# Expert weights of a hybrid encoder layer: one stream in long rows instead of 384 separate blocks

## The chip, the cores and the metric

The kernel runs on one core of one Trainium2 chip. A core has a matrix engine (PE, with its weight loads shown apart as PEld), a vector engine (DVE), a scalar engine (ACT), GpSimd (POOL), a sync engine (SP) that here mostly issues transfers, and 16 DMA engines that move data between HBM and the on-chip memory of 128 partitions. The metric is the device time of one execution in microseconds, lower is better. Before the change the runs gave 1816.92, 1818.54 and 1820.82 us, with a median of 1818.54 us.

## What is computed

One layer of a bidirectional encoder on 256 tokens of width 2048, all in float32. A mixing part (a Hyena group, a grouped-query attention group, an output projection) is followed by a layer norm, and then by 16 experts, each of which picks its own 32 tokens. The weights of the experts are most of the data: 16 experts x 3 matrices x 2048 x 1536 x 4 bytes are 604 MB, and each is used once.

```python
x = layer_norm(DN_ALPHA * x + jnp.einsum('ble,ed->bld', mixed, w_out), ln1_g, ln1_b)
# expert_choice_moe:
aff = jax.nn.softmax(logits, axis=-1)
gate, idx = lax.top_k(aff.transpose(0, 2, 1), C)          # C = 32 tokens for each expert
xg = x[bi, idx]
h = jax.nn.silu(jnp.einsum('becd,edf->becf', xg, w_gate)) * jnp.einsum('becd,edf->becf', xg, w_up)
y = jnp.einsum('becf,efd->becd', h, w_down) * gate[..., None]
return jnp.zeros_like(x).at[bi, idx].add(y.astype(x.dtype))
# and last
x = layer_norm(DN_ALPHA * x + moe, ln2_g, ln2_b)
```

## The kernel before

**Stages.** Up to about 400 us the mixing part runs: projections with PE busy nearly all the time, whose weights (`win`, `wo`) come through a ring of three slots (`ring_a`). Then come the moments of the first layer norm (`moments`, L739), the router's softmax (L759 to 768), the search for the top 32 (L790 to 801) and the one-hot matrices (`onehot`). From about 415 us the 16 experts follow (`expert`, L885): gate and up (`proj`, L867), then down (the loop from L917), and at the end the second layer norm.

**Blocks.** The weights of the experts are cut into blocks of [128, 3072] float32, 1.5 MB each: 8 for gate, 8 for up and 8 for down of each expert, 24 x 16 = 384. One block is one DMA: each of the 128 partitions gets one contiguous row of 12 KB. PE reads a gate or up block with 8 matmuls of 32x384 for each of two row pairs (L881; the profile counts 16), a down block with 12 (L929, counted 24) and then 2 (L936, counted 4). On odd experts the gathers of the next pair (L831) stand between the down blocks.

**Slots.** A block goes into a slot that `slot()` (L161) takes in turn from a list of 13: four of `ring_b`, four of `ring_d`, three of `ring_a`, two of `ring_c` (L736). The 14th place of the first round is half of a `big` buffer (`extra`, L718). Each pool turns over its own buffers: a new tile waits until PE has read the old one. Two other users take slots too. `row_tiles` (L838) puts two rows of the first layer norm into one, and `rw` (L952), the rows of the second layer norm for the end of the program, holds one of `ring_a`'s three from its allocation ahead of the last expert until the end.

**Order.** All weight DMAs stand on SP's queue (L592, L653, L875, L923, L925). SP works strictly in order: where one DMA waits for its slot, all behind it wait too. There are eight completion semaphores for DMAs of SP, used in turn, so that the ninth DMA also waits until the first has landed. The last down block of the last expert is fetched in two halves of 512-byte pieces (L923).

```python
rings[:] = [ring_b] * RB + [ring_d] * RD + [ring_a] * RA + [ring_c] * RC_
...
rw = slot(FR)[:, :D]
...
w = slot()
Q.dma_start(w, a[nm][e, s])
```

Of the kernel before, what the change touches and what calls it, by code (L numbers as in the profile page):

```python
# [10 lines left out]
F32 = mybir.dt.float32  # L11
FR = mybir.dt.float32r
AF = mybir.ActivationFunctionType
# [3 lines left out]
D = 2048  # L17
# [11 lines left out]
OUT_CHUNKS = [(0, 384), (384, 384), (768, 384), (1152, 384), (1536, 256), (1792, 256)]  # L29
EG = 2  # L30
MAGIC = 12582912.0
KL = OUT_CHUNKS[-1][0] // 128
RA = 3
RB = 4
RD = 4
RC_ = 2
NSPLIT = 4
AHEAD = 2
FSTEP = 3
EXTRA = 4  # L40
ROPE_LAG, SOFT_LAG = 3, 2
# [4 lines left out]
def constants():  # L46
# [31 lines left out]
    return np.ascontiguousarray(mix), np.ascontiguousarray(embt), np.ascontiguousarray(base)  # L78


def layout(i):
# [34 lines left out]
    for g in (n["q_norm"], n["k_norm"]):  # L116
# [11 lines left out]
                                for a, b in OUT_CHUNKS], 2))  # L128
    for k in ("w_gate", "w_up"):
        o[k] = c(n[k].reshape(E, 8, 2, 128, FF).transpose(0, 1, 3, 2, 4).reshape(E, 8, 128, SLOT))  # L130
    o["w_down"] = c(n["w_down"].reshape(E, 12, 128, 8, 256).transpose(0, 3, 2, 1, 4).reshape(E, 8, 128, SLOT))
    o["rows"] = c(np.stack([n["ln1_g"], n["ln1_b"], n["ln2_g"], n["ln2_b"]]).reshape(1, 4 * D))
# [3 lines left out]
ORDER = ["mixc", "base", "xt", "xr", "win", "bqkv", "par", "nrm", "ffn", "emb", "w3", "dec", "wo",  # L136
         "w_gate", "w_up", "w_down", "rows"]


def body(tc, a, out, upto=None):  # L140
# [7 lines left out]
    per = main.enter_context(tc.tile_pool(name="per", bufs=1, side="left"))  # L148
    ring_a = main.enter_context(tc.tile_pool(name="ra", bufs=RA, side="left"))
    s1b = ExitStack()  # L150
# [6 lines left out]

    rings = [ring_a]
    state = {"n": 0}

    def slot(dt=F32):  # L161
        p = rings[state["n"] % len(rings)]
        state["n"] += 1
        return p.tile([128, SLOT], dt, name="w", tag="w")

# [420 lines left out]

    pre = {}

    def ahead(pool):
        i = len(pre)  # L590
        w = pre["w_gate", i] = pool.tile([128, SLOT], F32, name="w", tag="w")
        Q.dma_start(w, a["w_gate"][0, i])  # L592

    gts, done = {}, set()
# [12 lines left out]
    for i in range(NCT + 4):  # L607
        if i == 1:
            Q.dma_start(wt[1][1], a["win"][1, 1])
        elif i:  # L610
            load_win(i)
        if i == NCT - 1:
            rope_tables()
        if i < NCT:
            side.append(first_filters() if i == 0 else filters(i))
        box = []
        for _ in hy_proj(i, box) if i < NCT else qkv_proj(i - NCT, box):
            tick()
        while len(side) > (1 if i == 0 else 0) and i < NCT + 3:
            tick()  # L620
        side.append(hy_mix(i, box) if i < NCT else qkv_post(i - NCT, box))
        if i == NCT:
            s1h.close()
            ring_b = main.enter_context(tc.tile_pool(name="rb", bufs=RB, side="right"))
        elif i > NCT:
            ahead(ring_b)
    res = big().rearrange("p (t d) -> p t d", t=2)
# [70 lines left out]
    for half in (0, 1):  # L698
        for ci, (c0, cn) in enumerate(OUT_CHUNKS):
            if half == 1 and ci == 0:  # L700
                while side:
                    tick()
                token_rms(sqa, 1)
                s1a.close()
                ring_d = main.enter_context(tc.tile_pool(name="rd", bufs=RD, side="right"))
            ps = [bank([128, 512], f"ip{t}") for t in range(2)]
# [6 lines left out]
            if half == 0 and ci == 0:  # L713
                ahead(ring_b)
            if half == 0 and ci == 3:
                room = big()
                spare = room[:, SLOT:].rearrange("p (n t) -> p n t", t=L)
                extra = pre["w_up", EXTRA] = room[:, :SLOT]  # L718
                Q.dma_start(extra, a["w_up"][0, EXTRA])
            for t in range(2):  # L720
# [145 lines left out]

    def proj(e, nm, tag, step=None):  # L867
        xg = xgs[e // EG]
        c0 = (e % EG) * CAP
        p = bank([128, 512], tag)  # L870
        for s in range(8):
            w = pre.pop((nm, s), None)
            if w is None:
                w = slot()
                Q.dma_start(w, a[nm][e, s])  # L875
            if step:
# [8 lines left out]
    def expert(e):  # L885
        step = None
        if e == 0:
# [7 lines left out]
        pg_ = proj(e, "w_gate", "ip0", step)  # L895
        h = pm_.tile([128, 384], F32, name="h")
        S.activation(h, pg_, AF.Silu)  # L897
        pu_ = proj(e, "w_up", "ip1")
        V.tensor_tensor(h, h, pu_, op=ALU.mult)  # L899
# [15 lines left out]
        acc = accs[0]  # L915
        last = e == n_exp - 1
        for n in range(8):  # L917
            w = slot()
            pieces = [(0, 128), (128, 256)] if last and n == 7 else [(0, 256)]
            for a0, a1 in pieces:  # L920
                c3 = lambda v: v.rearrange("p (b c) -> p b c", c=256)[:, :, a0:a1]
                if len(pieces) > 1:
                    Q.dma_start(c3(w), c3(a["w_down"][e, n]))  # L923
                else:
                    Q.dma_start(w, a["w_down"][e, n])  # L925
                py = bank([128, L])[:, :a1 - a0]
                for c in range(3):
                    for j in range(4):
                        T.matmul(py[32 * j:32 * j + 32, :], hT[:, c, 32 * j:32 * j + 32], c3(w)[:, 3 * j + c, :],  # L929
                                 start=c == 0, stop=c == 2)  # L930
# [13 lines left out]
            if e % EG == EG - 1 and e + 1 < E:  # L944
                for k in (2 * n, 2 * n + 1):
                    gather(e // EG + 1, k)

    for e in range(n_exp):
        if e == n_exp - 1:
            room = big().rearrange("p (z d) -> p z d", d=D)  # L950
            st, gb = room[:, 0], room[:, 1]
            rw = slot(FR)[:, :D]  # L952
            G.memset(st, 0.0)  # L953
            for p0, r0, rn in ((0, 2, 2), (2, 2, 1), (32, 2, 2)):
                Q.dma_start(st[p0:p0 + rn, :], a["rows"].rearrange("o (r d) -> (o r) d", d=D)[r0:r0 + rn, :])
            S.activation(rw, st, AF.Copy)
            V.tensor_tensor(rw[32:34], st[32:34], rw[32:34].bitcast(F32), op=ALU.subtract)
            for q in range(4):
# [22 lines left out]
    for t in range(2):  # L981
        for q in range(4):
            cs = slice(q * 512, (q + 1) * 512)
            p = bank([128, 512])
            T.matmul(p, lead[:, t, :], rw[0:34, cs], start=True, stop=True)
            V.scalar_tensor_tensor(acc[:, t, cs], acc[:, t, cs], mv[:, 3, t:t + 1], p, op0=ALU.mult, op1=ALU.add)
# [25 lines left out]
```

## Time and profile before

| what | value |
|---|---|
| runs | 1816.92, 1818.54, 1820.82 us (median 1818.54) |
| span of the profiled execution | 1814.5 us |
| median less this span | 4.0 us |
| PE, DVE, ACT, POOL busy | 72%, 26%, 18%, 6% of the span |
| DMA moved | 673.23 MB, mean 371 GB/s |
| DMA on the chain that ended last | 62% of the span |

The profile gives no time of its own for the profiled execution beside its span; the runs are 4.0 us longer in the median, which is what lies around the span. The profile has a page in parts: busy time of each engine, the span in 40 slices, the DMA queues, the chain that ended last, the costliest groups of instructions, and the DMA issues. The trace behind it answers questions on one stretch, one engine or one line. "idle 0.63 <- DMA" behind an instruction means that its engine stood idle for 0.63 us ahead of it and that a DMA ended this.

### The profile page before, as it was taken

To read this page: it belongs to the slowest core of one execution; us is meant where nothing else is said; L and a number is where in the kernel's file an instruction comes from. 1 tells how busy PE (TensorE), PEld (TensorE's weight loads), DVE (VectorE), ACT (ScalarE), POOL (GpSimd) and SP (SyncE) were. 2 spreads that over 40 slices of the span, in tenths; PEclk is the share of its full clock that TensorE was granted. 3 is DMA by queue.
4 is the path that set the end of the run, shared out by engine and by line. 5 is a ranking of instruction groups with operands and counts; after the bars stand their busy time and mean duration, and the time that the engine had idled before them with its cause. 6 is when DMAs were issued, how large, how long until landed. Compare 5 with 4: busy or idle time off the path is not lost.

```text
span 1814.5 us, 25770 instructions
## 1 busy us (share of the span) xinstructions
PE 1304.2 (72%) x11092; PEld 771.8 (43%) x11092; DVE 472.3 (26%) x937; ACT 321.3 (18%) x652; POOL 102.9 (6%) x142
## 2 busy tenths in 40 slices
PE   9999999999876647555756574657475867485845
PEld 7899999984332213221413141314131533141313
DVE  7988877553110001010101010101010101020105
ACT  6555457431000001000100010001000100010100
POOL 1334221000000000000000000000000000000000
PEclk9999999999979898998989799889887598897888
DMA  9344385658999999999999999999999999999987
GB/s 344 139 135 157 140 323 200 265 212 335 425 426 427 427 427 427 426 428 427 427 426 427 427 425 428 426 427 427 427 427 426 427 427 427 427 426 427 417 365 286
DMA packets 71080, 673.23 MB, mean 371 GB/s; under 512 B 7825, under 2 KB 11698, under 8 KB 17586
## 3 DMA queue, kind: packets, MB, share of 16 engines
q1 hardware_dynamic: 70838, 671.56, 89.2%
q8 instruction: 88, 1.44, 0.3%
q14 instruction: 26, 0.20, 0.0%
q0 software_dynamic: 128, 0.02, 0.0%
HBM read 669.45 MB, written 2.10 MB: 370 GB/s over the span
## 4 chain that ended last, share of the span: by engine, by line
DMA 62%; PE 19%; issue 10%; DVE 5%; ACT 1%; POOL 0%; POOLq 0%; DVEq 0%; SPq 0%; ACTq 0%
DMA w<-in_w_up_dram 21%; DMA w<-in_w_gate_dram 21%; DMA w<-in_w_down_dram 19%; PE ip L663 1%; PE ip L665 1%; PE ip L664 1%; PE ip L881 1%; PE ip L545 1%; PE ip L546 1%; PE ip L547 1%; DVE sl L226 1%; PE m L929 1%; PE ip L348 1%; PE ip L347 1%; PE ip L349 1%
## 5 line engine op out<-in xcount | busy, mean ns | idle before, releaser
L881 PE MATMUL ip<-w,xg 128*32 128x384 f32 x4080 | 459.5, 580 | 369.5 <-DMA w<-in_w_up_dram 213.1
L881 PEld LDWEIGHTS ip<-w,xg 128*32 128x32 f32 x4080 | 121.4, 121 | 691.5 <-DMA w<-in_w_up_dram 321.6
L929 PE MATMUL m<-w,hT 128*32 128x256 f32 (+1 forms) x3096 | 207.3, 403 | 33.0 <-DMA w<-in_w_down_dram 28.2
L899 DVE TENSOR_TENSOR h<-h,ip 128x384 f32<-128x384 f32 x16 | 8.9, 554 | 802.6 <-PE ip L881 802.6
L936 PE MATMUL m<-ys,sc 128*128 128x256 f32 (+1 forms) x516 | 151.1, 417 | 71.5 <-ACT ys L932 71.5
L937 DVE TENSOR_TENSOR big<-big,m 128x512 f32<-128x512 f32 x129 | 88.2, 684 | 410.5 <-PE m L936 410.5
L226 DVE TENSOR_TENSOR sl<-w,sh 128x768 fp32r<-128x768 f32 (+1 forms) x144 | 139.9, 976 | 48.9 <-ACT sh L225 48.5
L936 PEld LDWEIGHTS m<-ys,sc 128*128 128x128 f32 x516 | 90.4, 196 | 144.9 <-ACT ys L932 137.5
L929 PEld LDWEIGHTS m<-w,hT 128*32 128x32 f32 x3096 | 97.6, 114 | 109.5 <-PE m L936 33.8
L225 ACT ACTIVATE sh<-w 128x768 fp32r<-128x768 f32 (+1 forms) x144 | 117.5, 818 | 108.1 <-PE ip L664 45.9
L545 PE MATMUL ip<-big,sh 128*128 128x256 f32 x384 | 110.6, 289 | 1.0 <-ACT sh L225 1.0
L546 PE MATMUL ip<-big,sh 128*128 128x256 f32 x384 | 106.9, 279 | 0.0
L547 PE MATMUL ip<-big,sl 128*128 128x256 f32 x384 | 106.2, 279 | 0.8 <-DVE sl L226 0.8
L932 ACT ACTIVATE ys<-m 128x256 f32<-128x256 f32 x129 | 49.2, 381 | 297.9 <-PE m L929 297.9
L914 ACT ACTIVATE hT<-m 128x384 f32<-128x384 f32 x16 | 7.8, 490 | 465.8 <-PE m L912 457.3
L831 PEld LDWEIGHTS m<-oh,big 128*128 128x128 f32 x512 | 71.0, 203 | 7.8 <-issue 4.2
L545 PEld LDWEIGHTS ip<-big,sh 128*128 128x128 f32 x384 | 72.6, 189 | 2.8 <-ACT sh L225 2.2
L546 PEld LDWEIGHTS ip<-big,sh 128*128 128x128 f32 x384 | 72.3, 188 | 0.9 <-issue 0.2
L547 PEld LDWEIGHTS ip<-big,sl 128*128 128x128 f32 x384 | 72.0, 188 | 1.5 <-DVE sl L226 1.2
L897 ACT ACTIVATE h<-ip 128x384 f32<-128x384 f32 x16 | 7.8, 490 | 354.5 <-PE ip L881 354.5
L953 POOL MEMSET big<- 128x2048 f32 x1 | 1.8, 1804 | 1200.1 <-PE m L831 1200.1
L831 PE MATMUL m<-oh,big 128*128 128x64 f32 x512 | 68.7, 280 | 0.4 <-DVE oh L814 0.4
(225 smaller groups left out, 1304.7 us busy)
## 6 DMA issues: line engine op xcount, KB each, us to landing
w<-in_w_gate_dram SPq DMA_DIRECT2D x128, 1536.0 KB, 29.3
w<-in_w_up_dram SPq DMA_DIRECT2D x127, 1536.0 KB, 29.4
w<-in_w_down_dram SPq DMA_DIRECT2D x127, 1536.0 KB, 29.4
w<-in_win_dram SPq DMA_DIRECT2D x21, 1536.0 KB, 6.4
w<-in_wo_dram SPq DMA_DIRECT2D x8, 1536.0 KB, 8.6
w<-in_wo_dram SPq DMA_DIRECT2D x4, 1024.0 KB, 4.8
w<-in_win_dram SPq DMA_DIRECT2D x10, 384.0 KB, 5.7
xs<-in_xt_dram SPq DMA_DIRECT2D x8, 256.0 KB, 5.7
```

The source lines that it names most:

```text
L225: S.activation(h[:, :n], src, AF.Copy)
L226: V.tensor_tensor(l[:, :n], src, h[:, :n].bitcast(F32), op=ALU.subtract)
L347: T.matmul(o, xh[:, k, ts_], h[:, c], start=k == 0, stop=False)
L545: T.matmul(o, h[:, c], xh[:, k, :], start=k == 0 and j != 1, stop=False, skip_group_check=True)
L546: T.matmul(o, h[:, c], xl[:, k, :], start=False, stop=False, skip_group_check=True)
L547: T.matmul(o, l[:, c], xh[:, k, :], start=False, stop=k == KD - 1, skip_group_check=True)
L831: T.matmul(pt, xn[:, t, k * 128:(k + 1) * 128], ohs[g][:, t].rearrange("p e c -> p (e c)"), start=t == 0, stop=t == 1)
L881: T.matmul(p[32 * j:32 * j + 32, :384], xg[:, k, c0:c0 + CAP], w[:, kk * FF + j * 384:kk * FF + (j + 1) * 384], start=k == 0, stop=k == KD ...
L929: T.matmul(py[32 * j:32 * j + 32, :], hT[:, c, 32 * j:32 * j + 32], c3(w)[:, 3 * j + c, :], start=c == 0, stop=c == 2)
L932: S.activation(ys, py, AF.Copy)
L936: T.matmul(po[:, t, :], sc[:, t * 128:(t + 1) * 128], ys, start=True, stop=True)
L937: V.tensor_tensor(acc[:, :, ds_], acc[:, :, ds_], po, op=ALU.add)
```

## The change

The host lays all expert weights into one array `ws`, in the order in which they are used and cut into segments of one to four blocks. Within a segment each partition's blocks lie side by side, so that a segment of four is one DMA of 128 rows of 48 KB, one of three has rows of 36 KB. `plan()` lists the segments: each has a home, a place in it and a length. The homes `b` and `d` are standing buffers of four blocks; the left side, where `ring_a` and `ring_c` lay, becomes after the first round a third standing buffer `l` of six blocks, filled as two times three, and at the close four single slots `m`. A cycle is four, four, three and three blocks. `ring_c` gets a third slot, so that the first round has 15 places and not 14. `rw` lies beside the four slots of `m`; the rows of the first layer norm get a tile of their own and are fetched from ACT's queue and no longer from POOL's. The last block is laid out in two halves on the host.

```diff
+FIRST = [("b", 0), ("b", 1), ("b", 2), ("b", 3), ("d", 0), ("d", 1), ("d", 2), ("d", 3),
+         ("a", 0), ("a", 1), ("a", 2), ("c", 0), ("x", 0), ("c", 1), ("c", 2)]
+SECOND = [("b", 0, 1), ("b", 1, 1), ("b", 2, 2), ("d", 0, 2), ("d", 2, 2), ("l", 0, 3), ("l", 3, 3)]
+CYCLE = [("b", 0, 4), ("d", 0, 4), ("l", 0, 3), ("l", 3, 3)]
+CLOSING = [("b", 0, 4), ("d", 0, 4)] + [("m", z, 1) for z in range(4)] + [("b", z, 1) for z in range(4)] + [
+    ("d", z, 1) for z in range(3)]
...
+def plan():
+    segs = [(u, 1, home, r) for u, (home, r) in enumerate(FIRST)]
+    turns = list(SECOND)
+    while len(FIRST) + sum(n for _, _, n in turns + CLOSING) < E * NU:
+        turns += CYCLE
...
-    rings = [ring_a]
-    state = {"n": 0}
...
+    def source(u, m, c0, cn):
+        ws = a["ws"]
+        return bass.AP(tensor=ws.tensor, offset=ws.offset + u * 128 * SLOT + c0, ap=[[m * SLOT, 128], [1, cn]])
+
+    def fetch(k):
+        u, m, home, r = segs[k]
+        if home == "l" and "l" not in homes:
+            s0.close()
+            homes["l"] = s1.enter_context(tc.tile_pool(name="rl", bufs=1, side="left")).tile(
+                [128, 6 * SLOT], F32, name="wl")
+        if home == "m" and "m" not in homes:
+            s1.close()
+            homes["m"] = main.enter_context(tc.tile_pool(name="rm", bufs=1, side="left"))
...
+        if u + m == E * NU:
+            for z in range(2):
+                h = SLOT // 2
+                Q.dma_start(w[:, z * h:(z + 1) * h], source(u, m, z * h, h))
+        else:
+            Q.dma_start(w[:, :m * SLOT], source(u, m, 0, m * SLOT))
+
+    def weights(e, z, s):
+        u = (e * 3 + z) * 8 + s
+        if u not in held:
+            fetch(holds[u])
+        return held.pop(u)
...
-    pm_ = main.enter_context(tc.tile_pool(name="pm", bufs=1, side="left"))
-    ring_c = main.enter_context(tc.tile_pool(name="rc", bufs=RC_, side="left"))
-    rings[:] = [ring_b] * RB + [ring_d] * RD + [ring_a] * RA + [ring_c] * RC_
-    state["n"] = len(pre) - 1
+    pm_ = main.enter_context(tc.tile_pool(name="pm", bufs=1, side="right"))
+    homes["c"] = s0.enter_context(tc.tile_pool(name="rc", bufs=3, side="left"))
...
-        rows = slot()
+        rows = pm_.tile([128, 1024], F32, name="rows")
         for z in range(4):
-            G.dma_start(rows[32 * z:32 * z + 1, :1024], a["rows"][:, r0 * D + z * 1024:r0 * D + (z + 1) * 1024])
+            S.dma_start(rows[32 * z:32 * z + 1, :1024], a["rows"][:, r0 * D + z * 1024:r0 * D + (z + 1) * 1024])
...
+        if last:
+            rw.append(homes["m"].tile([128, D], FR, name="rw", bufs=1))
+            S.activation(rw[0][0:34], st[0:34], AF.Copy)
...
-            rw = slot(FR)[:, :D]
...
-    nc = _bacc.Bacc("TRN2", target_bir_lowering=False, num_devices=1)
+    nc = _bacc.Bacc("TRN2", target_bir_lowering=False, num_devices=1, dynamic_dma_scratch_size=1024)
```

The built programs show what moves. First SP's queue where the first round of expert blocks ends and the next begins (`w` are slots of the rings, `wb`, `wd` and `wl` the standing buffers; the last number is the row in elements). Before:

```order
79 L875 DMA w<-in_w_gate_dram 128x3072
80 L875 DMA w<-in_w_up_dram 128x3072 x7
81 L925 DMA w<-in_w_down_dram 128x3072 x8
82 L875 DMA w<-in_w_gate_dram 128x3072 x8
83 L875 DMA w<-in_w_up_dram 128x3072 x8
```

And with the change:

```order
79 L214 DMA wd<-in_ws_dram 128x3072
80 L214 DMA w<-in_ws_dram 128x3072 x6
81 L214 DMA wb<-in_ws_dram 128x3072 x2
82 L214 DMA wb<-in_ws_dram 128x6144
83 L214 DMA wd<-in_ws_dram 128x6144 x2
84 L214 DMA wl<-in_ws_dram 128x9216 x2
85 L214 DMA wb<-in_ws_dram 128x12288
86 L214 DMA wd<-in_ws_dram 128x12288
```

Before, five of the seven up DMAs in row 80 go to free slots and the last two go round to the first slots of `ring_b`; now six go to free slots of the left side.

Then ACT's queue at the first layer norm and the softmax (`big<-big,mv` writes a normalised quarter row of the tokens, `aff<-aff` is the exponential of the softmax, `xg` the first gathers). Before:

```order
272 L676 ACTIVATE big<-m 128x256 x2
273 L772 ACTIVATE big<-big,mv 128x512
274 L765 ACTIVATE aff<-aff 128x32
275 L772 ACTIVATE big<-big,mv 128x512 x7
276 L834 ACTIVATE xg<-m,par 128x64 x8
```

And with the change:

```order
272 L890 DMA rows<-in_rows_dram 1x1024
273 L726 ACTIVATE big<-m 128x256 x2
274 L821 ACTIVATE big<-big,mv 128x512 x3
275 L814 ACTIVATE aff<-aff 128x32
276 L821 ACTIVATE big<-big,mv 128x512 x5
277 L890 DMA rows<-in_rows_dram 1x1024 x3
278 L883 ACTIVATE xg<-m,par 128x64 x8
```

The exponential now stands behind three of the eight activations and not behind one, and four DMA issues are new on ACT.

Last, SP's queue at the end of the program. Before:

```order
127 L875 DMA w<-in_w_gate_dram 128x3072 x8
128 L875 DMA w<-in_w_up_dram 128x3072 x8
129 L925 DMA w<-in_w_down_dram 128x3072 x7
130 L923 DMA w<-in_w_down_dram 128x12x128 x2
131 L987 DMA out_dram<-big 128x512 x8
```

And with the change:

```order
160 L214 DMA wl<-in_ws_dram 128x9216
161 L214 DMA wb<-in_ws_dram 128x12288
162 L214 DMA wd<-in_ws_dram 128x12288
163 L214 DMA w<-in_ws_dram 128x3072 x4
164 L214 DMA wb<-in_ws_dram 128x3072 x4
165 L214 DMA wd<-in_ws_dram 128x3072 x2
166 L212 DMA wd<-in_ws_dram 128x1536 x2
167 L1031 DMA out_dram<-big 128x512 x8
```

The last eleven blocks stay single, and the last one comes in rows of 6 KB where there were pieces of 512 bytes.

## Rows read from the trace of the kernel before

**Rows 1.** The page's 40 slices (45 us each), and its shares of the last chain.

```profile
PEclk9999999999979898998989799889887598897888
GB/s 344 139 135 157 140 323 200 265 212 335 425 426 427 427 427 427 426 428 427 427 426 427 427 425 428 426 427 427 427 427 426 427 427 427 427 426 427 417 365 286
DMA 62%; PE 19%; issue 10%; DVE 5%; ACT 1%; POOL 0%; POOLq 0%; DVEq 0%; SPq 0%; ACTq 0%
```

**Rows 2.** Chain that ended last, 480 to 620 us: start us, us, what.

```profile
490.47 29.19 DMA w<-in_w_up_dram
519.72 29.45 DMA w<-in_w_down_dram
549.24 29.28 DMA w<-in_w_gate_dram
```

**Rows 3.** Waits of SP, whole span: total us, times, longest us.

```profile
SPq L925 <- DMA w<-in_w_up_dram: 377.0, 114, 4.7
```

**Rows 4.** Stretches: us, busy PE, PEld, DVE, ACT, POOL, PEclk, DMA share, GB/s.

```profile
14.00:18.00 4.00, 4.00 (x38) 4.00 (x37) 3.94 (x9) 2.85 (x5) 0.00 (x0) 1.00 1.04 412
18.00:26.00 8.00, 8.00 (x76) 7.70 (x75) 6.79 (x14) 4.69 (x10) 0.00 (x0) 1.00 1.04 423
410.00:420.00 10.00, 8.71 (x74) 6.30 (x73) 5.41 (x17) 1.77 (x4) 0.99 (x1) 1.00 0.16 45
465.00:1690.00 1225.00, 781.12 (x7236) 340.41 (x7234) 109.12 (x222) 83.63 (x210) 1.80 (x1) 0.88 1.01 427
1741.00:1757.00 16.00, 7.36 (x68) 1.84 (x64) 0.00 (x0) 0.00 (x0) 0.00 (x0) 0.84 0.64 254
1792.50:1797.50 5.00, 3.42 (x52) 2.08 (x52) 3.29 (x7) 0.66 (x2) 0.00 (x0) 1.00 0.94 226
```

**Rows 5.** Order of time, 403 to 420 us: SP's next issue, PE's first gathers and block.

```profile
414.63 2.19 PE L831 MATMUL m<-oh,big 128*128 128x64 f32 x18 [0.41 <-DVE oh L814]
...
416.75 1.50 PE L881 MATMUL ip<-w,xg 128*32 128x384 f32 x16
...
418.31 0.33 SPq L875 DMA_DIRECT2D w<-in_w_up_dram  x1
```

**Rows 6.** Order of time, 403 to 420 us: ACT and DVE around the softmax.

```profile
404.66 0.81 ACT L772 ACTIVATE big<-big,mv 128x512 f32<-128x512 f32 x1 [1.36 <-DVE mv L747]
...
405.17 0.19 DVE L764 TENSOR_TENSOR aff<-aff,sm 128x32 f32<-128x32 f32 x1
405.40 0.23 ACT L765 ACTIVATE aff<-aff 128x32 f32<-128x32 f32 x1
405.53 5.03 ACT L772 ACTIVATE big<-big,mv 128x512 f32<-128x512 f32 x7
```

**Rows 7.** Waits of SP from 1690 us to the end.

```profile
SPq L875 <- DMA w<-in_w_up_dram: 25.4, 1, 25.4
```

**Rows 8.** Order of time on PE, 1700 to 1782 us.

```profile
1750.68 1.53 PE L881 MATMUL ip<-w,xg 128*32 128x384 f32 x16 [2.13 <-DMA w<-in_w_up_dram]
1754.32 2.79 PE L881 MATMUL ip<-w,xg 128*32 128x384 f32 x16 [2.11 <-DMA w<-in_w_up_dram]
```

**Rows 9.** Order of time on PE, 1775 to 1815 us.

```profile
1793.09 1.50 PE L929 MATMUL m<-w,hT 128*32 128x256 f32 x24 [0.63 <-DMA w<-in_w_down_dram]
...
1796.20 0.86 PE L929 MATMUL m<-w,hT 128*32 128x128 f32 x24
...
1798.31 0.86 PE L929 MATMUL m<-w,hT 128*32 128x128 f32 x24
```

**Rows 10.** Order of time on PE, 1590 to 1612 us.

```profile
1592.37 2.78 PE L929 MATMUL m<-w,hT 128*32 128x256 f32 x24 [0.58 <-ACT hT L914]
...
1599.68 1.13 PE L936 MATMUL m<-ys,sc 128*128 128x256 f32 x4 [0.56 <-ACT ys L932]
1600.65 1.00 PE L831 MATMUL m<-oh,big 128*128 128x64 f32 x8
1601.58 1.50 PE L929 MATMUL m<-w,hT 128*32 128x256 f32 x24
```

More of the change, by code (lines that the diff above doesn't have):

```diff
@@ L33 @@
 RA = 3
-RB = 4
-RD = 4
-RC_ = 2
 NSPLIT = 4
@@ L78, in constants @@
     return np.ascontiguousarray(mix), np.ascontiguousarray(embt), np.ascontiguousarray(base)
+def plan():
[3 more added lines that the diff above has]
+        turns += CYCLE
+    u = len(FIRST)
+    for home, r, n in turns + CLOSING:
+        segs.append((u, n, home, r))
+        u += n
+    assert u == E * NU
+    return segs
 def layout(i):
@@ L148, in body @@
     per = main.enter_context(tc.tile_pool(name="per", bufs=1, side="left"))
-    ring_a = main.enter_context(tc.tile_pool(name="ra", bufs=RA, side="left"))
+    s0, s1 = ExitStack(), ExitStack()
+    ring_a = s0.enter_context(tc.tile_pool(name="ra", bufs=RA, side="left"))
     s1b = ExitStack()
@@ L156, in body, with slot @@
     psum = main.enter_context(tc.tile_pool(name="psum", bufs=2, space=bass.MemoryType.PSUM))
-    rings = [ring_a]
-    state = {"n": 0}
[L161 to L164, printed above, removed]
+    def slot():
+        return ring_a.tile([128, SLOT], F32, name="w", tag="w")
+    homes = {}
+    segs = plan()
+    holds = {u + z: k for k, (u, m, _, _) in enumerate(segs) for z in range(m)}
+    held = {}
+    def source(u, m, c0, cn):
[10 more added lines that the diff above has]
+            homes["m"] = main.enter_context(tc.tile_pool(name="rm", bufs=1, side="left"))
+        if home in ("a", "c", "m"):
+            p = ring_a if home == "a" else homes[home]
+            w = p.tile([128, SLOT], F32, name="w", tag="w", bufs=4 if home == "m" else None)
+        elif home == "x":
+            w = homes["x"]
+        else:
+            w = homes[home][:, r * SLOT:(r + m) * SLOT]
+        for z in range(m):
+            held[u + z] = w[:, z * SLOT:(z + 1) * SLOT]
+        if u + m == E * NU:
+            for z in range(2):
+                h = SLOT // 2
+                Q.dma_start(w[:, z * h:(z + 1) * h], source(u, m, z * h, h))
+        else:
+            Q.dma_start(w[:, :m * SLOT], source(u, m, 0, m * SLOT))
[4 more added lines that the diff above has]
+        return held.pop(u)
     def bank(shape, tag="m"):
@@ L623, in body @@
             s1h.close()
-            ring_b = main.enter_context(tc.tile_pool(name="rb", bufs=RB, side="right"))
+            homes["b"] = main.enter_context(tc.tile_pool(name="rb", bufs=1, side="right")).tile(
+                [128, 4 * SLOT], F32, name="wb")
         elif i > NCT:
-            ahead(ring_b)
+            fetch(i - NCT - 1)
     res = big().rearrange("p (t d) -> p t d", t=2)
@@ L704, in body @@
                 s1a.close()
-                ring_d = main.enter_context(tc.tile_pool(name="rd", bufs=RD, side="right"))
+                homes["d"] = main.enter_context(tc.tile_pool(name="rd", bufs=1, side="right")).tile(
+                    [128, 4 * SLOT], F32, name="wd")
             ps = [bank([128, 512], f"ip{t}") for t in range(2)]
@@ L713, in body @@
             if half == 0 and ci == 0:
-                ahead(ring_b)
+                fetch(3)
             if half == 0 and ci == 3:
@@ L871, in proj @@
         for s in range(8):
[L872 to L875, printed above, removed]
+            w = weights(e, z, s)
             if step:
```

45 lines of the change are left out of this document (20 added, 25 removed).

## The prediction

> **What bounds the kernel now.** I began with the page: from slice 11 (about 450 us) to slice 37 the DMA moves 425 to 428 GB/s without a dip, and 62% of the last chain is DMA [rows 1]. The chain of waits between 480 and 620 us has no engine in it, only DMA links that follow each other, 29.2 to 29.5 us each [rows 2]; eight blocks of 1.573 MB in 29.4 us are 428 GB/s. SP's longest wait in total is on the landing of the DMA eight places before, 114 times [rows 3]: eight are always in flight, so the DMA engines never lack work there. The stretch of 1225 us in [rows 4] says it once more: DMA share 1.01, 427 GB/s, PE busy in 781 of 1225 us. So for 1300 us only two things count: how fast the DMA engines work off a byte, and whether they ever run dry. They run dry twice: at 410 to 420 us (45 GB/s) and at 1741 to 1757 us (254 GB/s) [rows 4]. The change touches all three.
>
> **Part 1, the place more in the first round.** At 410 to 420 us the DMA moves 45 GB/s: 10 x (1 - 45/427) = 8.9 us are empty. All 14 places are full, and the next DMA leaves at 418.31 us, when PE has read the first block (PE's block begins at 416.75 and ends at about 418.25) [rows 5]. A 15th place lets one block of 1.573 MB / 427 GB/s = 3.68 us move within this hole, and the hole is longer than that. Against it: the restart comes later. The exponential of the softmax now stands behind three ACT instructions and not one. Eight of these take 0.72 us apiece in a row (5.03 for seven, [rows 6]). The first starts 0.15 us earlier at best, at 404.5 us, and three end at 404.5 + 2.16 = 406.66; the exponential was ready to run at 405.36 and ran at 405.40. So it is 1.26 us late, and everything from it to the first gather is one chain. PE has two counted gather matmuls fewer ahead of the first block (18 in 2.19 us, so 0.24 us back) [rows 5]. Net: 3.68 - 1.26 + 0.24 = **2.7 us** gained. The ends: nothing, if the late restart costs as much as the block gives, and 3.7. After that restart the segments of one, one, two, two, two and three times three blocks are each asked for by PE's reading with at least one other DMA still in flight, so I add nothing there. The four ACT issues for the layer norm rows replace four on POOL; SP shows 0.33 us for one issue [rows 5], they stand ahead of the activations (ACT waits there 1.36 us anyway) and behind them, where ACT idles until the first gather comes: nothing. If that cover is gone, 1.3 us.
>
> **Part 2, the slot that the last rows held.** From 1690 us on SP has one wait of 25.4 us on an up DMA [rows 7]. The code explains it: `rw` keeps one of `ring_a`'s three buffers to the end, three up blocks of the last expert are assigned to `ring_a`, and with two buffers left the third of them must wait until PE has read the first of them, which itself has only just landed. Everything behind it on SP waits too, the eight in flight run out, and from 1741 to 1757 us the DMA moves 254 GB/s: 16 x (1 - 254/427) = **6.5 us** lost [rows 4], and PE waits for DMA right up to there [rows 8]. With the change `rw` is no user of a weight slot. This comes back whole, unless the close finds another stall (a rival). Ends: 0 and 6.5.
>
> **Part 3, long rows.** If a row costs a fixed time c beside its bytes, fewer and longer rows save c each. No row over 16 KB is in the program before, so the price must come from short ones. From 14 to 18 us the DMA carries rows of 2 and 3 KB (mean 2.5 KB) at share 1.04 and 412 GB/s: 16 x 1.04 / 412 = 0.0404 ns per byte for one engine. In the expert stage, rows of 12 KB: 16 x 1.01 / 427 = 0.0378 [rows 4]. The difference, 0.0025, over (1/2560 - 1/12288) = 0.000309 gives c = 8 ns. From 18 to 26 us, where longer rows are mixed in, the same sum gives 4.8 ns (423 GB/s) [rows 4]. The pieces of 512 bytes at 1792.5 us give 16 x 0.94 / 226 x 512 = 34 ns each, 15 above the 19 that their bytes cost [rows 4], but these also jump about in the source. I take **8 ns**: those rows are nearest in length and alone in their stretch. An engine carries 8 of the 128 rows of a block. In segments of four blocks that is 2 rows per block in place of 8, 6 x 8 = 48 ns saved; in threes 2.67, 43 ns; in twos 4, 32 ns. `plan()` has 50 fours (200 blocks), 50 threes (150), 3 twos (6) and 28 singles: 9.6 + 6.4 + 0.2 = **16.2 us**. Ends: 0 (a row costs its bytes alone) and 30 (15 ns); 4.8 ns would give 9.7.
>
> [...]
>
> **What stays.** In the last block the 512-byte pieces become rows of 6 KB. They ran at 226 GB/s, but the last two pieces of PE's work start at 1796.20 and 1798.31 us right behind PE's own work, 3.1 and 5.2 us after the block before, which waited for its DMA [rows 9]: nothing gained there. The copy of the last rows on ACT moves to the last expert's down stage, where PE waits for DMA: nothing; 2 us if that cover were gone. The 21.4 us from 1793.09 to the end stay.
>
> **Sum.** 2.7 + 6.5 + 16.2 = 25.4 us off the span of 1814.5 us, which gives 1789.1; the runs lie 4.0 above the span, so 1793.1 against the median of 1818.54. A measurement tells 0.2% (3.6 us) from no change.
>
> **Why coarser fetches should not starve the DMA.** A home is asked for anew when all of its blocks are read. At that moment the other homes, 10 blocks or 36 us, are queued or moving. PE reads four blocks that have landed together in 6 us (1.50 us a gate or up block, [rows 8]), or, down with gathers, in 16 us: a block that begins 1.50 + 0.56 us ahead of 1599.68 and is followed at 1601.58 takes 3.96 us [rows 10]. Lag and burst together stay well under 36 us.
>
> **Rivals.**
> 1. *Long rows save nothing* (the row is cut into shorter pieces, or the bytes alone bind). For it: no row over 16 KB has run. Against: the short rows cost more per byte [rows 4]. Time: 1793.1 + 16.2 = 1809.3. Chance 0.11.
> 2. *A new stall at the close.* The first single slot `m` waits until PE has read both threes on the left side, and all of SP stands behind it, as it stood behind `rw`'s slot. If eight blocks in flight do not cover this, up to the old 6.5 us are lost: 1799.6. Against: eight blocks are 29 us, a burst of three takes under 10. Chance 0.06.
> 3. *PE becomes the bound, slower than before.* PE now waits for 14.7 us segments and works in bursts. [...] Chance 0.05. [...]
>
> **Numbers.** Forecast 0.78 with its own range 1790 to 1800, the rivals 0.11, 0.06 and 0.05. The low end, 1787, allows c of about 11 ns; the high end, 1804, takes 4.8 ns together with most of the stall at the close. Outside are rivals 1 and 3 and a little below: 0.17 to 0.2. Faster by over 0.2%: 0.93 (forecast, rivals 1 and 2, less a little for both at once); within 0.2%: 0.02; slower: 0.05.
>
> **What would show it.** The expert stage at about 432 GB/s and links of 3.64 us a block: part 3; 427 again would be rival 1. No wait of SP beyond 15 us near the end and no dip in GB/s ahead of the last slice: part 2. A hole of about 6.5 us instead of 8.9 near 415 us, with the exponential at about 406.7: part 1. Dips in the stream while PE is busy at a granted clock near 0.5 would prove me wrong by rival 3.

## The result and the profile after

| | before | after |
|---|---|---|
| median of the runs, us | 1819.68 (1816.92 to 1822.72, 4 runs) | 1798.13 (1797.27 to 1798.69, 4 runs) |
| ratio, 95% interval | 1 | 0.9883 [0.9869, 0.9897] |
| span of the profiled execution, us | 1814.5 | 1796.3 (its own time 1798.05) |
| DMA packets of the program | 71080 | 31706 |

The change is faster by 21.5 us (18.7 to 23.8 by the interval). Forecast were 25.4 us and 1793.1: the time lies inside the range of 1787 to 1804, and the gain is 4 us short. (The profiled execution's own time, 1798.05 us, is 1.8 above its span. So of the 4.0 us that stood between the median and the span before, only about 1.8 lie around a span, as in the other runs; the rest says that the execution profiled before was one of the faster ones. The forecast does not change by it, since the gain was taken off the median as well.)

The page of the changed kernel, the lines of [rows 1]:

```profile
PEclk9999999999875887978677888788887978788888
...
GB/s 348 114 156 165 141 295 211 241 216 345 437 435 429 430 431 433 433 434 432 433 433 429 431 431 433 434 433 433 431 433 431 431 431 434 435 428 435 429 427 231
...
DMA 44%; PE 21%; issue 10%; ACT 1%; DVE 1%; POOL 0%; POOLq 0%; DVEq 0%; ACTq 0%
```

The stage moves mostly 429 to 435 GB/s (single slices 427 to 437) in place of 425 to 428, and the dip that stood in the 39th slice (365) is gone. Less of the last chain is DMA: PE's work now comes in bursts, and parts of the bursts stand in the chain.

Stretches of the changed kernel (us, busy PE, PEld, DVE, ACT, POOL, PEclk, DMA share, GB/s), the first three as in [rows 4]:

```profile
410.00:420.00 10.00, 8.28 (x56) 7.05 (x58) 7.78 (x25) 3.16 (x6) 0.86 (x1) 1.00 0.65 274
465.00:1690.00 1225.00, 820.05 (x7294) 384.92 (x7294) 110.43 (x224) 85.03 (x212) 1.80 (x1) 0.81 1.00 432
1741.00:1757.00 16.00, 11.41 (x139) 4.65 (x132) 1.65 (x4) 0.87 (x2) 0.00 (x0) 0.99 1.01 428
1760.00:1765.00 5.00, 3.90 (x52) 2.31 (x52) 3.29 (x8) 0.38 (x1) 0.00 (x0) 1.00 0.97 399
1765.00:1770.00 5.00, 3.39 (x37) 1.98 (x31) 2.60 (x5) 0.77 (x2) 0.00 (x0) 1.00 0.58 242
1770.00:1775.00 5.00, 3.42 (x35) 1.87 (x37) 2.79 (x5) 0.38 (x1) 0.00 (x0) 1.00 0.49 204
1775.00:1780.00 5.00, 3.99 (x60) 2.52 (x56) 3.36 (x8) 0.66 (x2) 0.00 (x0) 1.00 0.19 77
```

The stage is at 432 GB/s, and the stretch that ran at 254 runs at 428. The new thing is the end: from about 1765 to 1777 us the share is one half. The DMA does not stop at once; half of the 16 engines are done some 11 us before the others. A share of one half alone could also be 16 engines that are busy half of the time, but the trace's packet records, which give each packet's start, length and size, exclude this: from 480 to 1690 us exactly 16 packets are under way in 97% of the time, and from 1768 to 1776.5 us exactly 8 in 89% of it. The kernel before shows no such stretch at its end.

SP's waits of the changed kernel from 1690 us on (total us, times, longest us), against [rows 7]:

```profile
SPq L1031 <- DVE big L1030: 33.3, 8, 31.6
SPq L214 <- PE ip L927: 13.6, 4, 7.7
SPq L214 <- PE m L975: 12.0, 1, 12.0
```

These are its three longest sums; the first is the wait for the output, and no fetch waits longer than 12.0 us, where one had waited 25.4. PE's last blocks of the changed kernel, against [rows 9]:

```profile
1774.82 1.50 PE L975 MATMUL m<-wd,hT 128*32 128x256 f32 x24 [0.52 <-DMA wd<-in_ws_dram]
...
1777.94 0.86 PE L975 MATMUL m<-wd,hT 128*32 128x128 f32 x24
...
1779.90 0.86 PE L975 MATMUL m<-wd,hT 128*32 128x128 f32 x24
```

From 1774.82 to the end are 21.5 us, as the 21.4 before. All of the gain lies ahead of this point.

### The profile page after: what moved, and what is told of

The parts are those of the page before. It is cut to its first block, busy times and chain, and to the rows that moved or that the text cites. A ratio compares the mean times of both kernels' runs of the same rounds, so it can differ in the third digit from the quotient of the medians.

```text
span 1796.3 us, 25177 instructions
## 1 busy us (share of the span) xinstructions
PE 1337.7 (74%) x11092; PEld 815.2 (45%) x11092; DVE 472.4 (26%) x937; ACT 321.8 (18%) x652; POOL 100.6 (6%) x138
## 2 busy tenths in 40 slices
DMA packets 31706, 673.16 MB, mean 375 GB/s; under 512 B 3652, under 2 KB 4453, under 8 KB 10601
## 4 chain that ended last, share of the span: by engine, by line
DMA 44%; PE 21%; issue 10%; ACT 1%; DVE 1%; POOL 0%; POOLq 0%; DVEq 0%; ACTq 0%
DMA wb<-in_ws_dram 32%; PE ip L927 8%; DMA wd<-in_ws_dram 7%; PE m L975 6%; DMA wl<-in_ws_dram 5%; PE m L982 4%; PE m L880 2%; ACT ys L978 1%; DVE big L1030 0%; DVE big L914 0%; PE m L958 0%; ACT hT L960 0%; DVE h L945 0%; DVE big L911 0%; POOL big L999 0%
## 5 line engine op out<-in xcount | busy, mean ns | idle before, releaser
L927 PE MATMUL ip<-wl,xg 128*32 128x384 f32 x1616 | 178.4, 589 | 91.7 <-DMA wl<-in_ws_dram 91.7
L927 PE MATMUL ip<-wd,xg 128*32 128x384 f32 x1152 | 136.7, 625 | 109.5 <-DMA wd<-in_ws_dram 109.5
L927 PE MATMUL ip<-wb,xg 128*32 128x384 f32 x1168 | 134.2, 604 | 107.5 <-DMA wb<-in_ws_dram 107.5
L982 PE MATMUL m<-ys,sc 128*128 128x256 f32 (+1 forms) x516 | 161.9, 441 | 59.2 <-ACT ys L978 59.2
L927 PEld LDWEIGHTS ip<-wl,xg 128*32 128x32 f32 x1616 | 58.0, 129 | 201.1 <-DMA wl<-in_ws_dram 102.8
L927 PEld LDWEIGHTS ip<-wd,xg 128*32 128x32 f32 x1152 | 43.1, 136 | 193.9 <-DMA wd<-in_ws_dram 109.3
L927 PEld LDWEIGHTS ip<-wb,xg 128*32 128x32 f32 x1168 | 42.7, 132 | 189.5 <-DMA wb<-in_ws_dram 109.4
L975 PE MATMUL m<-wb,hT 128*32 128x256 f32 x936 | 76.2, 471 | 28.8 <-DMA wb<-in_ws_dram 25.9
L975 PE MATMUL m<-wl,hT 128*32 128x256 f32 x1176 | 85.2, 429 | 13.0 <-DMA wl<-in_ws_dram 10.7
L601 PEld LDWEIGHTS ip<-big,sh 128*128 128x128 f32 x384 | 73.0, 190 | 2.2 <-ACT sh L281 1.5
```

The lines of the kernel that those rows point to most:

```text
L601: T.matmul(o, h[:, c], xh[:, k, :], start=k == 0 and j != 1, stop=False, skip_group_check=True)
L927: T.matmul(p[32 * j:32 * j + 32, :384], xg[:, k, c0:c0 + CAP], w[:, kk * FF + j * 384:kk * FF + (j + 1) * 384], start=k == 0, stop=k == KD ...
L982: T.matmul(po[:, t, :], sc[:, t * 128:(t + 1) * 128], ys, start=True, stop=True)
```

## The experiments

Two theories went into the runs. The first is the prediction's: place 2.7, pause 6.5, rows 16.2 us. The second was formed after the result, from the half share at the end: the DMA engines drift apart into two halves, the half behind sets the end, and the pause of the kernel before had let it catch up, so that taking the pause away gives back far less than 6.5 us. Ratios are to the kernel before on the same chip.

**The changed kernel again**, as the control of the runs with the exponential and the uneven rows.

> The changed kernel itself, on the same chip as the three that follow, so that they are compared with it and not only with the kernel before: 1798 us, ratio to before 0.988, as in its first timing.

Measured: 1796.7 us, 0.9877 [0.9863, 0.9890]. The two timings of the same kernel differ by 1.4 us; smaller differences than that say nothing below.

**The pause alone.** In the kernel before (with it, so that there is room, the rows of the first layer norm go to ACT's queue and the DMA scratch is cut to 1024, as in the changed kernel):

```diff
-            rw = slot(FR)[:, :D]
+            rw = pm_.tile([128, D], FR, name="rw")
```

> The kernel before, with one edit: the tile `rw` of the last expert's rows is a tile of its own and no longer takes a slot of the weight ring (to make room, the LN1 rows are fetched by ScalarE's queue). The pause of the fetch at 1741 to 1757 us goes. By the prediction's sum the pause costs 6.5 us: 1813 us (ratio to before 0.9964). By the theory formed after the result, that the 16 DMA engines have drifted into a half that is ahead and a half that is behind, and that only the half behind sets the end, which lacked work for 1.5 to 2 us: 1818 us (0.9990), and with the pause gone the DMA share at the end shows a step at one half for some 10 us, as in the changed kernel. If the pause cost nothing: 1819.7 (1.000).

Measured: 1818.99 us, 0.9994 [0.9984, 1.0003]: 1.1 us (-0.5 to 2.9). Its stretches:

```profile
1741.00:1757.00 16.00, 12.24 (x80) 2.59 (x72) 0.00 (x0) 0.00 (x0) 0.00 (x0) 0.56 1.01 427
1785.00:1790.00 5.00, 3.44 (x45) 2.07 (x48) 3.31 (x7) 0.38 (x1) 0.00 (x0) 1.00 0.51 214
```

The pause is filled completely, and the stretch at one half appears at the end, without long rows and without a new order of the fetches. That is the second theory's reading, and the 6.5 us of the first are excluded. One reservation: in this run's profile SP's first fetch of the expert stage after the hole left at 420.49 us, where it had been 418.31, and TensorE was at its lower level just ahead of it (granted clock 0.50 from 418 to 420 us); there is one profile of either kernel, so how often this happens in each is not known. If it were the rule here and never happened before, the pause would be worth 1.1 + 2.2 = 3.3 us, half of the 6.5. The kernel before, looked at more finely inside the pause, shows the same (same columns):

```profile
1745.00:1749.00 4.00, 1.50 (x16) 0.42 (x16) 0.00 (x0) 0.00 (x0) 0.00 (x0) 1.00 0.50 212
1751.00:1752.00 1.00, 1.00 (x16) 0.26 (x8) 0.00 (x0) 0.00 (x0) 0.00 (x0) 1.00 0.37 160
1752.00:1753.00 1.00, 0.21 (x4) 0.00 (x0) 0.00 (x0) 0.00 (x0) 0.00 (x0) 0.51 0.15 61
```

For most of the pause the share was one half and not nothing: the half behind still had work. It fell below only for 1 to 2 us. By the packet records an engine stood empty for 5.9 us in the mean of all 16 from 1741 to 1757 us. But only what is missing from 8 packets at a time is a loss of the half behind, and this comes to 1.1 us for each of its eight engines: the 1.1 us that the run gave back.

**Long rows alone.** In the changed kernel each segment is fetched block by block, into the same places:

```diff
-            Q.dma_start(w[:, :m * SLOT], source(u, m, 0, m * SLOT))
+            for z in range(m):
+                Q.dma_start(w[:, z * SLOT:(z + 1) * SLOT], source(u, m, z * SLOT, SLOT))
```

> The changed kernel, same places, same stream, same waits of the segments, but each segment of two, three or four blocks is fetched as so many DMAs of one block each, so that all rows are 12 KB again. If the long rows are worth what the packets' times say (a 12 KB row 460 ns, a 36 KB row 1364, a 48 KB row 1817: 8 ns of each packet saved, 8 rows a block on each engine, some 250 of 384 packets saved in each lane), the time goes back by 16 us: 1814 us (0.997 of before). If the gain of the change came from fewer fetches, fewer waits or the gone pause: 1798 us (0.988).

Measured: 1812.1 us, 0.9962 [0.9948, 0.9977]; against 0.9883 that is 14.4 us back. Its stage:

```profile
465.00:1690.00 1225.00, 796.10 (x7298) 345.19 (x7294) 110.45 (x224) 84.61 (x212) 1.80 (x1) 0.86 1.01 427
```

427 GB/s, the old rate, in the new program. The rows are the gain in the stage, and the order of the places is not. The run by itself leaves one rival: with the short rows it also has 385 weight DMAs for the experts again in place of 132, so the gain could lie in fewer DMAs. The packet records speak against it: the median packet takes 460 ns for 12 KB, 1364 for 36 KB and 1816 for 48 KB, so 8 short rows of a block are 48 ns dearer than 2 long ones and 43 dearer than 2.67, which makes 9.6 + 6.4 = 16 us for the fifty fours and fifty threes and leaves nothing for the number of DMAs.

**14 places.** `("c", 2)` is dropped from `FIRST`, the pool `rc` has two buffers, `CLOSING` ends with four single blocks in place of three.

> The changed kernel with 14 places in the first round: the third tile of the left ring is gone, and a 4th single block closes the list, so all 384 blocks are still fetched. One block more must be fetched after the weights begin to be used: by the price of a block in the stage, 3.65 us, 1801.8 us (0.9902 of before). If matrix work and not the fetch sets the end of the changed kernel, the time stays at 1798 us (0.988).

Measured: 1801.05 us, 0.9900 [0.9887, 0.9912], 3.1 us above the first timing of the changed kernel and 4.2 above the second: the block's price of 3.65 lies between. The fetch, not matrix work, sets the end.

**More code, on GpSimd.** After each expert's activation of the gate (but the last's):

```diff
+            G.tensor_copy(idle, h[:, :2])
+            for _ in range(500):
+                G.memset(idle, 0.0)
```

> The changed kernel with 7500 tiny memsets on GpSimd (500 after each expert's activation but the last's), which has nothing else to do there: 64 bytes of code each, 480 KB, some 29 packets of 16 KB of code to be loaded beside the 67 of the stage. If code loading puts one half of the DMA engines behind (67 packets of about 1.25 us on 8 engines give the 10 us of lag at the end), 29 more cost 3.6 packets of 1.25 us on each engine of that half: 1802.6 us (0.9907 of before), and the step at half share at the end grows to some 15 us. If the halves drift for another reason: 1798 us (0.988) and a step of 10 us.

Measured: 1826.57 us, 1.0040 [1.0028, 1.0052], 28 us slower, and it tells nothing of the halves. Page rows of this run (queue: packets, MB, share of 16 engines; and a group of instructions):

```profile
q8 instruction: 87, 1.43, 0.3%
q14 instruction: 79, 0.65, 0.1%
...
L950 DVE TENSOR_TENSOR h<-h,ip 128x384 f32<-128x384 f32 x16 | 8.9, 554 | 752.6 <-POOL idle L948 527.1
```

The code went to another queue, in packets of 8 KB: 79 there, 21 in the changed kernel, and the 58 more on 7515 instructions are 63 bytes each, where 64 were expected. The copy that was to pace them tied VectorE's product of `h` to GpSimd: 527 us of its idle time end with the memsets. That the late down blocks held up the fetch is my guess; from 465 to 1690 us the DMA moved 427 GB/s at a share of 1.00, where it had moved 432.

**Less code, on TensorE.**

```diff
-            for kk in range(2):
-                k = 2 * s + kk
-                for j in range(4):
-                    T.matmul(p[32 * j:32 * j + 32, :384], xg[:, k, c0:c0 + CAP], ...
+            j = s % 4
+            T.matmul(p[32 * j:32 * j + 32, :384], xg[:, 2 * s, c0:c0 + CAP], ...
...
-                for c in range(3):
-                    for j in range(4):
-                        T.matmul(py[32 * j:32 * j + 32, :], hT[:, c, 32 * j:32 * j + 32], wp[:, 3 * j + c, :], ...
+                for j in range(4):
+                    T.matmul(py[32 * j:32 * j + 32, :], hT[:, 0, 32 * j:32 * j + 32], wp[:, 3 * j, :], ...
```

> The changed kernel with two thirds of the experts' matmuls left out (of each gate and up block 1 of 8 matmuls is left, of each down block 4 of 12), so the output is not the reference's; all weights are fetched and each block is still released by a matmul that reads it. 2824 weight loads and as many matmuls fewer: 361 KB of TensorE's code, 22 of the 65 packets of 16 KB that the trace shows from 430 us on. If code loading puts one half of the DMA engines behind: 22 packets on 8 engines by 1.05 to 1.25 us each give 2.9 to 3.4 us back, 1794 us where the changed kernel has 1797 (0.986), and the stretch at half DMA share at the end shrinks by a third, from some 10 us to 7. If TensorE's own speed, and not the fetch, set the end: the stage of 1375 us would shrink far more, by tens of us. If code has nothing to do with the lag: 1797 us and a stretch of 10 us.

Measured: 1791.89 us, 0.9848 [0.9835, 0.9862]: 5 to 6 us under the changed kernel's two timings. Its page's row on that code, and its end in stretches:

```profile
q8 instruction: 43, 0.70, 0.2%
```

```profile
1760.00:1765.00 5.00, 3.60 (x17) 1.53 (x13) 2.38 (x5) 0.77 (x2) 0.00 (x0) 0.50 1.00 412
1765.00:1770.00 5.00, 4.45 (x15) 2.45 (x16) 2.31 (x5) 0.38 (x1) 0.00 (x0) 0.50 0.61 249
1770.00:1775.00 5.00, 4.09 (x26) 2.27 (x24) 3.47 (x8) 0.56 (x2) 0.00 (x0) 0.50 0.00 0
```

44 code packets fewer (87 to 43), twice what I had counted: 44 x 16384 bytes on 2824 matmuls are 255 bytes for a matmul and its weight load, not 128. A code packet took 1.05 us in the mean in the trace's packet records, so on 8 engines 44 x 1.05 / 8 = 5.8 us were to be had, and 5 to 6 came. The stretch below full share shrinks from some 11 us to 4.4 (1765.0 to 1769.4 in windows of 1 us). TensorE's granted clock was 0.55 in the stage (465 to 1690 us), and TensorE was still no bound: the DMA share there was 1.00, at 433 GB/s. So the lag follows the amount of TensorE's code. The packet records show it growing: where the stream passes from 36 KB to 48 KB rows, one sees when each engine gets there. From the 4th to the 13th of the 16 engines this took 1.3 us at 475 us, after 3 code packets since 430 us, and 11.6 at 1694 us, after 60; in this run, with the same rows, 1.2 after one and 4.0 after 20. That the packets fall on one half alone is inferred from the half share and these sizes; no record names a packet's engine.

**Rows moved to the half that is ahead.**

```diff
+UNEVEN = (46, 71, 95)
...
+        elif k in UNEVEN:
+            for p0, pn in ((0, 8), (8, 8), (16, 112)):
+                Q.dma_start(w[p0:p0 + pn, :m * SLOT], source(u, m, 0, m * SLOT, p0, pn))
...
```

> The changed kernel with three of its fifty segments of four blocks (at about a quarter, a half and three quarters of the list) fetched as three DMAs instead of one: rows 0 to 7, rows 8 to 15, and rows 16 to 127. A DMA of 8 rows can occupy only 8 engines; the tiny transfers of 1 and 2 rows near the end landed with the half of the engines that is ahead, so rows of such short DMAs should go to that half: it moves 9 rows of these segments and the other half 7. Each segment takes one 48 KB packet of 1.82 us from the half behind: 5.5 us in all, of a lag of 10.5 us. If the half behind sets the end: 1793 us (0.9856 of before), and the DMA share falls from full to nothing at the end with almost no step at one half. If the lag of that half is not what sets the end, or the rows go evenly: 1798 us (0.988). If the 8 rows go to the half behind: 1803 us (0.991) and a step of 21 us.

Measured: 1890.56 us, 1.0390 [1.0369, 1.0410]: 94 us slower, 31 for each of three segments, where a gain of 5 was expected. A stretch of it, in the same columns:

```profile
810.00:820.00 10.00, 0.00 (x0) 0.00 (x0) 0.00 (x0) 0.00 (x0) 0.00 (x0) 0.50 0.93 197
```

The engines are busy, but from 775 to 815 us a 48 KB packet takes 3.4 to 5.9 us, about two to three times the 1.82 of the other segments, with 16 packets under way all the time, so on all engines. Behind the expectation stands this: a row is one packet (6400 of 48 KB in the changed kernel, 128 for each of its fifty segments of four), so 8 rows can keep no more than 8 engines busy; and the five packets of the transfers of 1 and 2 rows near the end ran there from 1684.3 to 1686.8 us, in two of the chains of packets that pass to 48 KB rows first (eight from 1694.2 to 1698.0 us, the others from 1704.7 on). Where the 8 rows of this run went is not shown.

**The same three segments as two DMAs of 64 rows**: `((0, 64), (64, 64))` in the same place.

> The three segments that cost 94 us as 8, 8 and 112 rows, now as two DMAs of 64 rows each. If it was the DMAs of 8 rows, which cannot occupy all engines: no loss, 1797 us (0.988). If a row fetched by another engine than in the other segments is what slows the packets (1.82 us for 48 KB there became 3.6 to 5 us on all engines): a loss of the same order, some 30 us a segment, 1890 us.

Measured: 1867.25 us, 1.0257 [1.0238, 1.0277]: 23 us a segment. So DMAs of 8 rows are not needed for the loss: from 800 to 840 us the DMA moves 321 GB/s here, at a share of 0.97. That a DMA of part of the partitions slows the packets in flight beside it is my guess, and neither run isolates it. Half the rate in the three segments alone would not be enough: a segment would then lose its own 4 x 3.64 = 14.6 us, and 23 and 31 were lost. No record here names an engine, or says whether the 8 rows went to the half that is ahead.

**The exponential first.** The eight activations take their bias from a copy that is made after the softmax's sum:

```diff
+    mb = per.tile([128, 2], F32, name="mb")
+    V.scalar_tensor_tensor(mb, sm[:, :, 1], 0.0, mv[:, 4], op0=ALU.mult, op1=ALU.add)
...
-                         bias=mv[:, 4, t:t + 1], ...
+                         bias=mb[:, t:t + 1], ...
```

> The changed kernel with the eight normalizing activations bound to the sum of the softmax, so that ScalarE runs the exponential first, as in the kernel before. In the changed kernel the exponential ran at 408.75 us, 1.1 us after its input was ready (407.63), behind two of these activations. The chain from it to the first segment's fetch at 421.18 us moves up by 1.1 us, and with it all that follows in a stage that the fetch sets: 1797 us, 1.1 us (0.0006) under the changed kernel. If the chain has slack elsewhere, or the normalized rows then come too late for the first gather matmul: no gain, 1798 us.

Measured: 1804.92 us, 0.9926 [0.9912, 0.9939], 8 us slower than the control. In its order of time the exponential runs right behind its input:

```profile
408.60 0.19 DVE L813 TENSOR_TENSOR aff<-aff,sm 128x32 f32<-128x32 f32 x1
408.82 0.23 ACT L814 ACTIVATE aff<-aff 128x32 f32<-128x32 f32 x1 [2.33 <-DVE aff L813]
```

The chain did become 1.0 us shorter: from the router's logits (L736) to the transposes of the softmax 3.65 us (406.27 to 409.92) where the control takes 4.65 (403.10 to 407.75). But it began 3.2 us later, and TensorE ran at the lower level from 420 to 428 us:

```profile
420.00:424.00 4.00, 4.00 (x23) 1.67 (x22) 0.67 (x4) 0.41 (x1) 0.00 (x0) 0.50 0.00 0
424.00:428.00 4.00, 4.00 (x24) 1.53 (x20) 0.00 (x0) 0.41 (x1) 0.00 (x0) 0.50 0.63 215
```

**Both edits.**

> Both edits together, the exponential first and the three uneven segments: if both gains are real and independent, 1.1 + 5 us under the changed kernel, 1792 us (0.985 of before).

Measured: 1896.38 us, 1.0421 [1.0399, 1.0442]; the two losses stand beside each other.

**More warm-up**, `HOT2` 17 in place of 14 in the changed kernel.

> The changed kernel with 17 warm-up matmuls instead of 14 ahead of the slot matmuls of the routing: they end 1.3 us later, where TensorE stood idle for 1.32 us. In seven of nine profiles so far the granted clock fell to the lower level between 416 and 428 us, in the gap and the small matmuls before the first expert, and the first segment's fetch came 1.3 to 3 us later for it. If the gap is what lets the clock fall: 1.3 to 2 us faster than the changed kernel, 1795 us (0.987). If it falls anyway: 1797 us (0.9877).

Measured: 1796.9 us, 0.9880 [0.9863, 0.9897]. In its profile the clock did not fall (1.00 from 414 to 432 us), and the fetch began again at 419.29 us where the control's began at 420.80. The times of the two kernels don't differ. Inconclusive: 1.5 us is below what this comparison can tell.

**The exponential first, with 16 warm-ups.**

> The exponential first, as in the run that came out 8 us slower with the clock at its lower level from 418.5 to 428 us, and 16 warm-up matmuls instead of 14, which fill the 0.9 us that TensorE stood idle there. If that run lost by the clock alone: the first segment's fetch comes 1.1 us ahead of the changed kernel's without a fall of the clock, and 2.4 us ahead of the one with it: 1794 to 1796 us (0.986 to 0.987). If the exponential's order costs something else: again 1803 to 1805 us (0.992).

Measured: 1802.35 us, 0.9904 [0.9890, 0.9918]: slow again, and at the lower level again (0.50 from 420 to 428 us). So the clock was not the whole of it. A line of the early part, 60 to 300 us, in the control and, second, in this run:

```profile
L602 PE MATMUL ip<-big,sh 128*128 128x256 f32 x276 | 76.8, 278 | 0.0
```

```profile
L602 PE MATMUL ip<-big,sh 128*128 128x256 f32 x277 | 77.9, 281 | 0.0
```

The same matmuls, ahead of every edited line, take 1% longer; in the run with 14 warm-ups they take the same 281 ns. What both have is the new tile `mb` in `per`: 8 bytes a partition, 32 in the allocation, and in the built program all pools behind it on the left side, with the mixing part's weights and split tiles (`sh`, `sl`), begin 32 bytes later. A shift of these pools by itself is not the cause: the run with the memsets also adds a tile to `per` and moves the same pools by the same 32 bytes, and there the same matmuls (one line further down) take 278 ns:

```profile
L603 PE MATMUL ip<-big,sh 128*128 128x256 f32 x277 | 77.1, 278 | 0.0
```

Its tile stands ahead of `big` in `per` and moves `big` as well, where `mb` comes behind `big`; whether that matters was not tried. The expert stage of the runs with `mb` is slower too. DMA queue of the control and of the run with 14 warm-ups, 480 to 1690 us (packets, MB, share):

```profile
q1 hardware_dynamic: 13644, 521.68, 99.9%
```

```profile
q1 hardware_dynamic: 13575, 520.45, 99.9%
```

0.24% fewer bytes in the same time at the same share; the median 48 KB packet took 1819 ns in place of 1816, the median 36 KB packet 1367 in place of 1364. Over some 1350 us of stage that is 3.2 us, and 3.1 us were lost by 300 us (the matmul of L639 runs at 301.7 where the control has it at 298.6). The run with the memsets has the 1819 and 1367 ns as well, and none of the runs without a new tile in `per` has them. But the 48 KB segments go to `b` and `d`, which lie on the right side and do not move, so the address that a packet is written to is not the reason either. What costs these 3 ns stays open. A version with the exponential first and no new tile was not tried; the tile alone was not tried either.

## Why the prediction was right, and where it was wrong

| part | forecast, us | the runs |
|---|---|---|
| long rows | 16.2 | 14.4 by the run with short rows; 16.8 by the trace |
| 15th place, net | 2.7 | about 2.6: block 3.1 to 4.2, exponential -1.1 |
| pause | 6.5 | 1.1 (-0.5 to 2.9) |
| sum | 25.4 | 18 to 21; measured 21.5 (18.7 to 23.8) |

**Long rows: right.** From 480 to 1690 us the DMA moved 516.36 MB before and 522.82 MB after, 1.25% more, which on 369 blocks x 3.68 us = 1358 us of stage is 16.8 us. The 8 ns a row from the short rows of the start [rows 4] held beyond 12 KB: on one of 16 engines 4 x 12288 bytes at 427 GB/s and 49152 at 432 differ by 21 ns, 7 for each of the three rows saved. Rival 1 is refuted.

**The 15th place: right, in both of its terms.** The block is worth 3.65 us, and the exponential is late as reckoned:

```profile
406.62 1.52 ACT L821 ACTIVATE big<-big,mv 128x512 f32<-128x512 f32 x2 [1.29 <-DVE mv L796]
...
408.05 0.80 ACT L821 ACTIVATE big<-big,mv 128x512 f32<-128x512 f32 x1
...
408.75 0.21 ACT L814 ACTIVATE aff<-aff 128x32 f32<-128x32 f32 x1
```

These are ACT's rows of the changed kernel, as in [rows 6]; the input was ready at 407.63. In the control the exponential ran at 406.74, where 406.7 was forecast. The hole shrank about as forecast: from 400 to 440 us the DMA moved 291 GB/s before, 316 in the changed kernel and 309 in the control, which is 2.3 and 1.7 us at 432 GB/s where the forecast was a net 2.7. The restart at 421.18 us, 2.9 later than the 418.31 of [rows 5], looked worse than it is: 1.7 us of it came at 54 to 64 us, where the granted clock of that one execution fell to 0.83. The control has none of that; its restart at 420.80 has the lower level around 418 to 420 us instead.

**The pause: wrong by 5 us, and this is the step that failed.** The prediction took 16 x (1 - 254/427) for the loss. A mean share of 16 engines is time lost only if all of them stand still together, and they did not: for most of the pause one half worked on (share 0.50 from 1745 to 1749 us). What the end loses is what the half behind loses, and only from 1751 to 1753 us was the share clearly below one half (0.37 and 0.15). The pause had cost the half ahead the rest, which it had in hand. Without the pause the lead of some 11 us lasts to the end, where it shows as the stretch at one half. The cause named for the pause (`rw` holding a slot) and its disappearance were right. The time came out inside the range although this term was 5 us off, because the range had 11 us of room above the forecast; no second error made up for it.

**The rivals.** Rival 2, a new stall at the close, did not come: no fetch wait above 12.0 us, no dip ahead of the end. Rival 3, PE as the bound, did not come either, but it came nearer than I had reckoned. An odd expert's down blocks with gathers ran wholly at the lower level in places, as from 549 to 577 us, at a granted clock of 0.50 (changed kernel, order of time on PE):

```profile
549.32 2.79 PE L975 MATMUL m<-wb,hT 128*32 128x256 f32 x24
552.67 2.08 PE L982 MATMUL m<-ys,sc 128*128 128x256 f32 x4 [0.56 <-ACT ys L978]
554.54 1.81 PE L880 MATMUL m<-oh,big 128*128 128x64 f32 x8
556.28 2.79 PE L975 MATMUL m<-wb,hT 128*32 128x256 f32 x24
```

6.96 us a block, 27.8 for four, where the prediction had 16 and the fetch takes 14.6. Matmuls that take 2.79 us here took 1.50 at a granted clock of 1.00 (the block at 1774.82 us above). The 36 us of other segments in flight covered even that: the share stayed at 1.00, at 432 GB/s. The mean clock fell from 0.88 to 0.81, and the run with two thirds of the matmuls left out gained no more than its code packets were worth.

## What to carry to other kernels

A DMA share of one half need not be 16 engines that idle half of the time: here 8 packets were under way from 1768 to 1776.5 us, half of the engines was done, and the half behind set the end. Look for this, and price a pause by what the half behind lost, here 1.1 us where the mean share said 6.5. A row cost 7 to 8 ns here on top of its bytes, so even this saturated stream gained a per cent, 432 GB/s for 427, from rows of 36 and 48 KB in place of 12. Before splitting DMAs by partitions inside a full stream, time one of them: here a split segment cost 23 to 31 us. And time even a small edit, such as a new tile of 8 bytes, by itself: here one went with 5 to 8 us that nobody had planned.

## What was not expected of the hardware

- Code loading is on the path of this DMA-bound kernel: 44 code packets of 16 KB fewer made it 5 to 6 us faster, and the lag of one half fell from some 11 us to 4.4.
- Three segments of 6.3 MB fetched as 8, 8 and 112 rows cost 31 us each, as 64 and 64 rows 23 us each, with the engines busy all the while: a share of 0.93 to 1.08 at 168 to 223 GB/s (780 to 820 us) in the first, of 0.97 at 321 GB/s (800 to 840 us) in the second.
- A new tile of 8 bytes a partition goes with 3 ns on each 36 or 48 KB packet in all four runs that add one; `mb`, but not the tile of the memsets, also goes with 1% on the early matmuls. Together this is some 6 us. The cause is open: the standing buffers of the 48 KB packets do not move.
- TensorE's granted clock fell to 0.50 around the restart (from some point between 415 and 419 us on) in 11 of 14 profiles of the two kernels and their variants, each after a warm-up of 14 to 17 matmuls; the first fetch behind it came 1.5 us later in the control than in the run with three more warm-up matmuls, where it stayed at 1.00. Why it falls in one execution and not in the next stays open.
